# Norm rows through DRAM, scores behind a gate, and two moved steps in a one-core hybrid diffusion step

## The chip, the cores and the metric

The kernel runs on one core of a Trainium2 chip. The metric is the device time of one execution in microseconds; shown are the median and the range of several runs, and one further execution taken with the hardware profiler. The engines are TensorE (PE; its weight loads are listed apart as PEld), VectorE (DVE), ScalarE (ACT), GpSimd (POOL) and SyncE (SP), which issues nearly all DMAs.

## The reference, cut to what matters

One inference step of a two-layer backbone, width 1024, for 128 context tokens and 512 latent tokens that go through the same weights. Layer 0 mixes tokens by a bidirectional chunked scan with 32 heads in 4 groups, layer 1 by differential attention with 8 heads; a gated convolutional channel mixer follows each. All is fp32.

```python
def _rms(x):
    return x * lax.rsqrt(jnp.mean(x * x, axis=-1, keepdims=True) + EPS)

# end of the scan mixer: a norm over each group's 512 channels
y = y.reshape(b, l, SSD_INNER) * jax.nn.silu(z)
y = _rms(y.reshape(b, l, SSD_GROUPS, SSD_INNER // SSD_GROUPS)).reshape(b, l, SSD_INNER)
y = y * norm_g

# differential attention, per head, for a block of 128 queries
s = jnp.einsum('bqhcd,bkhcd->bhcqk', qi, k) * DA_SCALE      # c: two key maps of 64
p = jax.nn.softmax(s, axis=-1)
w = p[:, :, 0] - lam * p[:, :, 1]
o = jnp.einsum('bhqk,bkhd->bqhd', w, v)

# a norm over each head's 128 channels
o = _rms(o) * subln_g * (1.0 - lam_init)
```

Two kinds of norm matter here: that of the four scan groups and that of the eight attention heads. In both, one number per token multiplies all channels.

## The kernel before, in words

Activations lie transposed: channels on the 128 partitions, tokens along the free axis, 640 of them (512 latent, then 128 context). A dense product runs over units of weights: each unit is 128 output channels by 1024 inputs, loaded by SP into one of four raw buffers (L124), split by ScalarE into a rounded high part `whi` (L95) and by VectorE into a low part `wlo` (L101). A tile of 128 outputs takes eight steps of six matmuls (high by high, high by low, low by high, each over two token halves) into one of three wide PSUM buffers, tag "d", of two banks each.

All other work is written as Python generators that are advanced by a tick. Every dense step of six matmuls is a tick (`hook`); a generator that yields n is continued n ticks later. That gives the order in which instructions are written. A planner then orders them once more, outside the stretch at the start that is written under a manual schedule: of the instructions that it thinks ready (operands made, buffer free) an engine takes the one written first. Each engine then executes its own list strictly in that order.

The steps that the change touches:

- `rms_bcast` (L187) makes a norm's factor. Four matmuls of the squares against ones put the sums of 160 tokens each onto partition strips of 32 (tile `ms`); `rsqrt` (L172) takes the root in nine small VectorE operations (`rs_v`, `rs_a`, `rs_y`); after a wait of some ticks four fp32 matmuls against `sel`, columns with the value 0.375 that finish the root's scaling, spread the row to all partitions. The scan's groups write it into the wide buffer `gbc`, the heads into `obc`, the layers' own norms and the first one into `nbc`.
- `ssd_norm` (L877) and the end of `att_tail` (L1084) call it, and VectorE multiplies the data by the spread row and the gains (`svec` columns 16 on, `sg`).
- `att_head` (L1034) forms the scores `sl` of a block of 128 queries: twelve matmuls, six for each of the two key maps, from the high and low parts of q and k. Each map has its own wide buffer, and each uses one half of the array's rows. VectorE takes the maximum, ScalarE the exponential, which frees the buffer.
- `first_tiles` (L380), under the manual schedule, makes the first norm and, in `rows`, products of the condition vector with modulation weights (`modrow`) that arrive by DMA in parts `mp`. The row products of part 0 stand behind the spread of the first root.
- `ssd_dt` (L644) makes the step sizes of the scan and the running sums of the decays. Its rows (`rows`, from `dta`) are written to DRAM as `rowd` and read back, spread over the partitions, as `rb` by each chunk of the scan.

Of the kernel before, what the change touches and what calls it, by code (L numbers as in the profile page):

```python
# [9 lines left out]
F32 = mybir.dt.float32  # L10
# [3 lines left out]
AF = mybir.ActivationFunctionType  # L14
ALU = mybir.AluOpType
# [30 lines left out]
class Step:  # L46
# [140 lines left out]
    def rms_bcast(self, alloc, sq, t0, t1, count, wait=4):  # L187


        n = (t1 - t0) // 4  # L190
        ms = self.bank("m", "ms")
# [5 lines left out]
        self.rsqrt(y, ms[:, :n], n, count)  # L197
        yield wait
        bc = alloc()
        for j in range(4):  # L200
            self.mm(bc[:, j * n:(j + 1) * n], self.sel[:, j:j + 1].to_broadcast([P, P]), y, True, True)
        return bc

    def wide(self, name):
# [175 lines left out]
    def first_tiles(self, h, pool):  # L380
# [243 lines left out]
    def ssd_consts(self, pool):  # L624
        nc, a = self.nc, self.a
        t = lambda shape, name, dt=F32: pool.tile(shape, dt, tag=name, name=name, bufs=1)
        self.scw = t([P, 24, 4], "scw")
        nc.sync.dma_start(self.scw, a["scw"])
        nc.vector.tensor_scalar(self.scw, self.scw, 0.5, None, ALU.mult)
        self.svec = t([P, 32], "svec")  # L630
        nc.sync.dma_start(self.svec, a["svec"])
        self.dtb = t([P, 1], "dtb")
        nc.sync.dma_start(self.dtb, a["dtb"])
        self.fold = t([P, 64], "fold")
        nc.sync.dma_start(self.fold, a["fold"])
        self.ea = t([P, 64], "ea")
        nc.sync.dma_start(self.ea, a["alog"])
        self.act(self.ea, self.ea, AF.Exp)
        self.dt = t([P, NCH, 64], "dt")
        self.C = t([P, NCH, 64], "Ctok")  # L640
        self.wst = t([P, NCH, 64], "wst")
        self.cd = t([P, NCH, 64], "cd")

    def ssd_dt(self, ps):  # L644
# [229 lines left out]
        output(NL, ops)  # L874
        yield 1

    def ssd_norm(self, g, y):  # L877
# [12 lines left out]
    def ssd(self, h, dtps, nextnorm, pool):  # L890
# [4 lines left out]
        def finish(g):  # L895

            yield from self.ssd_group(g, xf[g], *bcs[g], pool)
            scanned[g] = True
            while len(zs[g]) < 4:
                yield 1  # L900
            for t in range(4):
                self.stt(xf[g][t], xf[g][t], 0.5, zs[g][t], ALU.mult, ALU.mult)
            yield 1
            yield from self.ssd_norm(g, xf[g])

        def z_tiles(g):
            for t in range(4):
# [46 lines left out]
    def att_consts(self, pool):  # L954
        nc, a = self.nc, self.a
        t = lambda shape, name, dt=F32: pool.tile(shape, dt, tag=name, name=name, bufs=1)
        self.rope = t([P, 2, TS], "rope")
        nc.sync.dma_start(self.rope, a["rope"])
        lv = t([P, 256], "lv")
        nc.sync.dma_start(lv, a["lam"])  # L960
        ls = t([P, 2], "ls")
        lj = t([P, 64], "lj")
        for i in range(2):
            nc.vector.tensor_tensor_reduce(lj, lv[:, 128 * i:128 * i + 64], lv[:, 128 * i + 64:128 * i + 128], 1.0, 0.0,
                                           ALU.mult, ALU.add, ls[:, i:i + 1])
# [4 lines left out]
        self.sg = t([P, 1], "sg")  # L970
        nc.sync.dma_start(self.sg, a["subg"])
        nc.vector.tensor_scalar(self.sg, self.sg, 1.0 - LAM_INIT, None, ALU.mult)

    def att_v(self, ps, hd, vs, pool):

        nc = self.nc
        x = self.slot("f", f"v{hd}", bufs=NF)
        self.act(x, ps[:, PO:PO + T], AF.Copy)
        hi = pool.tile([P, NCH, P], F32R, tag="vh", name=f"vh{hd}", bufs=2)
        lo = pool.tile([P, NCH, P], F32R, tag="vl", name=f"vl{hd}", bufs=2)  # L980
        vp = pool.tile([P, P], F32, tag="vp", name=f"vp{hd}", bufs=2)
# [14 lines left out]
        self.act(vp, pm[:, :P], AF.Copy)  # L996
        nc.sync.dma_start(self.a["vout"][:, hd * P:(hd + 1) * P], vp)

    def att_evac(self, ps, hd, name, pool):

        x = self.slot("f", f"{name}{hd}", bufs=NF)[:, :TS]
        p = pool.tile([P, TP], F32, tag=f"{name}p", name=f"{name}p{hd}", bufs=2)
        self.act(x, ps[:, PO:PO + TS], AF.Copy)
        self.act(p, ps[:, PO + TS:PO + T], AF.Copy, scale=DA_SCALE if name == "q" else 1.0)
        return x, p

    def att_rope(self, out, x):
# [7 lines left out]
    def att_q(self, x, hd, pool):  # L1015
# [5 lines left out]
        self.stt(lo, q, DA_SCALE, hi.bitcast(F32), ALU.mult, ALU.subtract)  # L1021
        return hi, lo

    def att_k(self, x, hd, pool):

# [5 lines left out]
        self.tt(lo, k, hi.bitcast(F32), ALU.subtract)  # L1031
        return hi, lo

    def att_head(self, hd, qp, kp, qs, k, vs, o, pool):  # L1034


        nc = self.nc
        (qh, ql), (kh, kl) = qs, k
        half = [slice(64 * m, 64 * m + 64) for m in range(2)]

        def softmax(s, n, m, st):
            e = self.slot("f", f"e{m}", bufs=NF)
            nc.vector.tensor_reduce(st[:, m:m + 1], s, AX.X, ALU.max, negate=True)
            self.act(e[:, :n], s, AF.Exp, bias=st[:, m:m + 1], accum_out=st[:, 2 + m:3 + m])
            return e

        def stats():
# [36 lines left out]
    def att_tail(self, hd, w, ws, vs, os_, pool):  # L1084
# [36 lines left out]
        sq = self.slot("sq", "osq", bufs=1)  # L1121
        self.act(sq, o, AF.Square)
        yield 2
        bc = yield from self.rms_bcast(lambda: self.wide("obc"), [sq], 0, T, P, 4 if hd == 7 else 7)
        self.stt(o, o, self.sg, bc[:, :T], ALU.mult, ALU.mult)

    def attention(self, h, nextnorm, pool):
        nc = self.nc
        self.cv = pool.tile([P, D], F32, tag="cv", name="cv", bufs=1)
        nc.sync.dma_start(self.cv, self.a["cv"])  # L1130
        o, tk, self.tails = [], [], {}
# [203 lines left out]
```

## Time and profile before

| | |
|---|---|
| median of 3 runs | 1892.9 us (1892.28 to 1893.92) |
| the profiled execution | 1892.41 us |
| its span, first to last instruction | 1890.6 us |
| mean granted TensorE clock | 0.994 |
| busy share: PE, DVE, ACT | 98%, 73%, 51% |
| DMA, mean over the span | 109 GB/s |

The profile lists for each engine the busy time, then groups of instructions by line, engine, operation and tile, with the idle time before them and what ended it. "out<-in" are the program's names, with the numbers of buffers left out. The chain that ended last follows, from the last instruction back, what released each one. A row of a stretch gives its bounds, its length, the busy time and count of PE, PEld, DVE, ACT and POOL in it, the granted clock, the share of the DMA engines and GB/s; where it is asked of one tile, the busy times are those of the instructions on that tile. A row in order of time gives the start, the length of the merged piece, the engine, the line, the operation and its count.

### The profile page before, as it was taken

What the parts mean: (1) busy time and instruction counts of PE and PEld (TensorE: products, weight loads), DVE (VectorE), ACT (ScalarE), POOL (GpSimd) and SP (SyncE); (2) the same over time, 40 slices, a digit from 0 to 9 for tenths busy, and PEclk for the clock granted to TensorE, in tenths of its full rate; (3) what the DMA queues carried; (4) which work ended last, traced back from release to release, by engine and by line L of the source; (5) the groups of instructions that cost most, each with busy time, mean ns of one, the idle gap of its engine ahead of it and who ended that gap; (6) DMA issues with size and microseconds to landing.
All of it is one profiled execution on the core that took longest, in us unless ns stands there. A gap on an engine that the chain in (4) does not pass through costs nothing.

```text
span 1890.6 us, 32986 instructions
## 1 busy us (share of the span) xinstructions
PE 1857.6 (98%) x13410; PEld 1763.2 (93%) x13410; DVE 1371.1 (73%) x2638; ACT 955.9 (51%) x1748; POOL 0.2 (0%) x4
## 2 busy tenths in 40 slices
PE   7999999999999999999999999999999999999997
PEld 5799999999999999999999988898899999999996
DVE  5689999999658999974455877888686543553554
ACT  3479696968336441442443656666446432441441
POOL 0000000000000000000000000000000000000000
PEclk9999999999999999999999999999999999999998
DMA  9844353526533557632222211111042222222211
GB/s 325 278 115 136 90 155 90 147 91 205 176 113 122 190 169 231 190 102 79 76 70 70 76 49 50 52 35 32 26 124 79 78 72 74 75 72 79 73 40 56
DMA packets 78056, 206.13 MB, mean 109 GB/s; under 512 B 9104, under 2 KB 15824, under 8 KB 77776
## 3 DMA queue, kind: packets, MB, share of 16 engines
q1 hardware_dynamic: 77328, 203.50, 34.3%
q8 instruction: 105, 1.72, 0.4%
q10 hardware_dynamic: 576, 0.52, 0.1%
q14 instruction: 47, 0.39, 0.1%
HBM read 198.06 MB, written 5.93 MB: 108 GB/s over the span
## 4 chain that ended last, share of the span: by engine, by line
PE 94%; DVE 3%; DMA 1%; ACT 1%; SPq 0%; issue 0%; DVEq 0%; ACTq 0%
PE up L104 31%; PE po L104 25%; PE z L104 6%; PE x L104 5%; PE st L104 5%; PE bc L104 3%; PE v L104 3%; PE yp L104 3%; PE q L104 2%; PE sl L104 2%; PE k L104 2%; PE ov L104 1%; PE modrow L104 1%; PE wt L1106 1%; PE in L104 1%; PE xtp L737 1%
## 5 line engine op out<-in xcount | busy, mean ns | idle before, releaser
L95 ACT ACTIVATE whi<-raw 128x1024 fp32r<-128x1024 f32 (+4 forms) x230 | 235.0, 1022 | 406.5 <-PE po L104 237.6
L101 DVE TENSOR_TENSOR wlo<-raw,whi 128x1024 fp32r<-128x1024 f32 (+3 forms) x229 | 269.6, 1178 | 177.4 <-ACT whi L95 171.6
L98 DVE SCALAR_TENSOR_TENSOR xr<-po,mod,xr 128x256 f32<-128x256 f32 (+2 forms) x231 | 88.7, 433 | 157.6 <-PE po L104 157.5
L104 PE MATMUL po<-mh,whi 128*128 128x256 f32 (+1 forms) x704 | 167.6, 310 | 0.0
L104 PE MATMUL po<-ml,whi 128*128 128x256 f32 (+1 forms) x704 | 167.4, 309 | 0.0
L104 PE MATMUL po<-mh,wlo 128*128 128x256 f32 (+1 forms) x704 | 167.1, 309 | 0.0
L104 PE MATMUL up<-h11h,wlo 128*128 128x256 f32 (+1 forms) x656 | 149.4, 309 | 0.0
L104 PE MATMUL up<-h01l,whi 128*128 128x256 f32 (+1 forms) x656 | 149.4, 309 | 0.0
L104 PE MATMUL up<-h11l,whi 128*128 128x256 f32 (+1 forms) x656 | 149.4, 309 | 0.0
L104 PE MATMUL up<-h11h,whi 128*128 128x256 f32 (+1 forms) x656 | 149.4, 309 | 0.0
L104 PE MATMUL up<-h01h,wlo 128*128 128x256 f32 (+1 forms) x656 | 149.4, 309 | 0.0
L104 PE MATMUL up<-h01h,whi 128*128 128x256 f32 (+1 forms) x656 | 149.4, 309 | 0.0
L104 PEld LDWEIGHTS po<-mh,whi 128*128 128x128 f32 x704 | 128.3, 188 | 0.6 <-ACT mh L95 0.4
L104 PEld LDWEIGHTS po<-mh,wlo 128*128 128x128 f32 x704 | 128.5, 188 | 0.0
L104 PEld LDWEIGHTS po<-ml,whi 128*128 128x128 f32 x704 | 128.4, 188 | 0.0
L104 PEld LDWEIGHTS up<-h01h,wlo 128*128 128x128 f32 x656 | 119.3, 188 | 0.0
L104 PEld LDWEIGHTS up<-h01h,whi 128*128 128x128 f32 x656 | 119.3, 188 | 0.0
L104 PEld LDWEIGHTS up<-h11h,wlo 128*128 128x128 f32 x656 | 119.3, 188 | 0.0
L104 PEld LDWEIGHTS up<-h11h,whi 128*128 128x128 f32 x656 | 119.3, 188 | 0.0
L104 PEld LDWEIGHTS up<-h01l,whi 128*128 128x128 f32 x656 | 119.2, 188 | 0.0
L104 PEld LDWEIGHTS up<-h11l,whi 128*128 128x128 f32 x656 | 119.2, 188 | 0.0
L98 DVE SCALAR_TENSOR_TENSOR ca<-uraw,fcw,ca 128x511 f32<-128x511 f32 (+1 forms) x176 | 85.2, 546 | 11.7 <-ACT ca L95 11.7
(496 smaller groups left out, 4385.6 us busy)
## 6 DMA issues: line engine op xcount, KB each, us to landing
raw<-in_w_up SPq DMA_DIRECT2D x88, 512.0 KB, 3.5
mw<-in_modT SPq DMA_DIRECT2D x48, 512.0 KB, 3.6
raw<-in_w_in SPq DMA_DIRECT2D x40, 512.0 KB, 5.1
rb<-rowd SPq DMA_DIRECT2D x40, 512.0 KB, 5.7
raw<-in_w_dn SPq DMA_DIRECT2D x32, 448.0 KB, 3.3
raw<-in_w_qkv SPq DMA_DIRECT2D x24, 512.0 KB, 3.5
mr<-in_mod SPq DMA_DIRECT2D x44, 256.0 KB, 5.3
mp<-in_modp SPq DMA_DIRECT2D x32, 256.0 KB, 5.4
```

The costliest lines, as they stand in the source:

```text
L95: return self.nc.scalar.activation(out, in_, func, **k)
L98: return self.nc.vector.scalar_tensor_tensor(out, in0, s, in1, op0, op1)
L101: return self.nc.vector.tensor_tensor(out, a, b, op)
L104: return self.nc.tensor.matmul(out, lhsT, rhs, start=start, stop=stop)
L737: tr = lambda out, x, c: nc.tensor.transpose(out, x[:, c * P:(c + 1) * P], self.ident)
L1106: nc.tensor.transpose(pm[:, b * P:(b + 1) * P], ws[b][:, kc * P:(kc + 1) * P], self.ident)
```

## The change

Four things are edited.

- A new `rms_spread` takes the place of `rms_bcast` in the four scan groups and in the first seven heads. It writes the row of roots from four partitions to a DRAM row and reads it back to all 128 partitions into an SBUF tile `rbc`; both DMAs are on SP. The factor 0.375 that `sel` had brought goes into the gains (`svec`, and a second column of `sg`; the last head keeps the matmuls and the old gain). The wait before the multiply is 8 ticks in the scan (4 before) and 9 in the attention (7 before).
- In `att_head` the first product of each map and column half of a block is made to depend on the latest copy out of a dense tile, the latest exponential, and the operations that made the low parts of q and k. Blocks start one tick later in all heads but the last.
- In `first_tiles` the row products of the first three of eight steps are written ahead of the spread of the first root.
- In `ssd_dt` the wait ahead of the decay rows is 12 ticks in place of 5.

```diff
+    def rms_spread(self, pool, sq, count, wait):
+
+        n = T // 4
+        y = self.rms_rows(sq, 0, n, count)
+        d = self.dram.tile([T], F32, tag="rsd", name="rsd", bufs=2)
+        self.nc.sync.dma_start(d.rearrange("(j n) -> j n", j=4), y.rearrange("(j r) n -> j r n", r=32)[:, 0, :])
+        bc = pool.tile([P, T], F32, tag="rbc", name="rbc", bufs=1)
+        self.nc.sync.dma_start(bc, d.partition_broadcast(P))
         yield wait
-        bc = alloc()
-        for j in range(4):
-            self.mm(bc[:, j * n:(j + 1) * n], self.sel[:, j:j + 1].to_broadcast([P, P]), y, True, True)
         return bc
...
+        rows(0, 0, 3)
         try:
             next(st)
...
-        rows(0, 0, KT)
+        rows(0, 3, KT)
...
+        nc.vector.tensor_scalar(self.svec[:, 16:], self.svec[:, 16:], 3.0 / 8, None, ALU.mult)
...
-        yield 5
+        yield 12
...
-        bc = yield from self.rms_bcast(lambda: self.wide("gbc"), [sq], 0, T, 512)
+        bc = yield from self.rms_spread(pool, [sq], 512, 8)
...
-        self.act(x, ps[:, PO:PO + T], AF.Copy)
+        self.held["evac"] = self.act(x, ps[:, PO:PO + T], AF.Copy)
...
+    def hold(self, i, gate):
+        for g in gate:
+            self.tc.add_manual_dep(i.ins, g.ins.name, mybir.DependencyInfo(
+                mybir.DependencyClass.Sync, mybir.DependencyReason.DATA), reason="scores")
...
-        yield 3 if last else 4
+        yield 3 if last else 5
...
+            gate = [*self.held.values(), *lows]
...
-                        self.mm(r[:, 192 + c0:192 + c0 + 320], x[hf, qb], kk[hf, c0:c0 + 320], j == 0, j == 2)
+                        i = self.mm(r[:, 192 + c0:192 + c0 + 320], x[hf, qb], kk[hf, c0:c0 + 320], j == 0, j == 2)
+                        if j == 0:
+                            self.hold(i, gate)
...
-        bc = yield from self.rms_bcast(lambda: self.wide("obc"), [sq], 0, T, P, 4 if hd == 7 else 7)
-        self.stt(o, o, self.sg, bc[:, :T], ALU.mult, ALU.mult)
+        if hd == 7:
+            bc = yield from self.rms_bcast(lambda: self.wide("obc"), [sq], 0, T, P, 4)
+        else:
+            bc = yield from self.rms_spread(pool, [sq], P, 9)
+        self.stt(o, o, self.sg[:, hd // 7:hd // 7 + 1], bc[:, :T], ALU.mult, ALU.mult)
```

The remaining edits hand the exponentials, the copies of q and k and the operations of the low parts on, so that `att_head` can name them.

More of the change, by code (lines that the diff above doesn't have):

```diff
@@ L190, in rms_bcast, with rms_rows @@
         n = (t1 - t0) // 4
+        y = self.rms_rows(sq, t0, n, count)
+        yield wait
+        bc = alloc()
+        for j in range(4):
+            self.mm(bc[:, j * n:(j + 1) * n], self.sel[:, j:j + 1].to_broadcast([P, P]), y, True, True)
+        return bc
+    def rms_rows(self, sq, t0, n, count):
         ms = self.bank("m", "ms")
@@ L197, in rms_bcast @@
         self.rsqrt(y, ms[:, :n], n, count)
+        return y
+    def rms_spread(self, pool, sq, count, wait):
[5 more added lines that the diff above has]
+        self.nc.sync.dma_start(bc, d.partition_broadcast(P))
         yield wait
-        bc = alloc()
-        for j in range(4):
-            self.mm(bc[:, j * n:(j + 1) * n], self.sel[:, j:j + 1].to_broadcast([P, P]), y, True, True)
         return bc
@@ L875, in ssd_group, with ssd_norm @@
         yield 1
-    def ssd_norm(self, g, y):
+    def ssd_norm(self, g, y, pool):
         sq = self.slot("sq", "gsq", bufs=1)
@@ L903, in finish @@
             yield 1
-            yield from self.ssd_norm(g, xf[g])
+            yield from self.ssd_norm(g, xf[g], pool)
         def z_tiles(g):
@@ L969, in att_consts @@
         nc.vector.tensor_scalar(self.nlam, self.nlam, -LAM_INIT, None, ALU.add)
-        self.sg = t([P, 1], "sg")
-        nc.sync.dma_start(self.sg, a["subg"])
-        nc.vector.tensor_scalar(self.sg, self.sg, 1.0 - LAM_INIT, None, ALU.mult)
+        self.sg = t([P, 2], "sg")
+        nc.sync.dma_start(self.sg[:, 1:], a["subg"])
+        nc.vector.tensor_scalar(self.sg[:, 1:], self.sg[:, 1:], 1.0 - LAM_INIT, None, ALU.mult)
+        nc.vector.tensor_scalar(self.sg[:, :1], self.sg[:, 1:], 3.0 / 8, None, ALU.mult)
     def att_v(self, ps, hd, vs, pool):
@@ L1003, in att_evac @@
         self.act(x, ps[:, PO:PO + TS], AF.Copy)
-        self.act(p, ps[:, PO + TS:PO + T], AF.Copy, scale=DA_SCALE if name == "q" else 1.0)
+        self.held["evac"] = self.act(p, ps[:, PO + TS:PO + T], AF.Copy, scale=DA_SCALE if name == "q" else 1.0)
         return x, p
@@ L1020, in att_q @@
         self.act(hi, q, AF.Copy, scale=DA_SCALE)
-        self.stt(lo, q, DA_SCALE, hi.bitcast(F32), ALU.mult, ALU.subtract)
-        return hi, lo
+        i = self.stt(lo, q, DA_SCALE, hi.bitcast(F32), ALU.mult, ALU.subtract)
+        return hi, lo, i
     def att_k(self, x, hd, pool):
@@ L1030, in att_k @@
         self.act(hi, k, AF.Copy)
-        self.tt(lo, k, hi.bitcast(F32), ALU.subtract)
-        return hi, lo
+        i = self.tt(lo, k, hi.bitcast(F32), ALU.subtract)
+        return hi, lo, i
     def att_head(self, hd, qp, kp, qs, k, vs, o, pool):
         nc = self.nc
-        (qh, ql), (kh, kl) = qs, k
+        (qh, ql, i), (kh, kl, j) = qs, k
+        lows = i, j
         half = [slice(64 * m, 64 * m + 64) for m in range(2)]
@@ L1043, in softmax @@
             nc.vector.tensor_reduce(st[:, m:m + 1], s, AX.X, ALU.max, negate=True)
-            self.act(e[:, :n], s, AF.Exp, bias=st[:, m:m + 1], accum_out=st[:, 2 + m:3 + m])
+            self.held["exp"] = self.act(e[:, :n], s, AF.Exp, bias=st[:, m:m + 1], accum_out=st[:, 2 + m:3 + m])
             return e
@@ L1130, in attention @@
         nc.sync.dma_start(self.cv, self.a["cv"])
-        o, tk, self.tails = [], [], {}
+        o, tk, self.tails, self.held = [], [], {}, {}
         self.start_tiles(h)
```

## The prediction, made before the result was known

> **What bounds the kernel now.** I read the busy totals and the chain that ended last first, then the busy time by stretch of the stages that the change touches, then single tiles and the order in time around each edit.
>
> ```profile
> span 1890.6 us, 32986 instructions
> PE 1857.6 (98%) x13410; PEld 1763.2 (93%) x13410; DVE 1371.1 (73%) x2638; ACT 955.9 (51%) x1748; POOL 0.2 (0%) x4
> PE 94%; DVE 3%; DMA 1%; ACT 1%; SPq 0%; issue 0%; DVEq 0%; ACTq 0%
> ...
> 84.00:100.00 16.00, 16.00 (x114) 14.33 (x113) 7.00 (x12) 9.14 (x20) 0.00 (x0) 1.00 0.76 275
> ...
> 60.00:490.00 430.00, 428.29 (x3308) 391.14 (x3307) 393.54 (x798) 322.53 (x755) 0.00 (x0) 1.00 0.48 143
> 1040.00:1330.00 290.00, 288.13 (x1968) 257.58 (x1968) 227.53 (x471) 178.23 (x375) 0.00 (x0) 0.99 0.16 48
> ```
>
> TensorE carries 94% of the chain, and in the two stages that the change edits (the scan, 60 to 490 us; the attention, 1040 to 1330 us) it is busy all but 1.7 and 1.9 us. A microsecond of TensorE work taken out there is a microsecond of the time, unless VectorE, 78% busy in the attention and 92% in the scan, becomes late. So I count TensorE time and then look for what VectorE's order could give back.
>
> **Part 1, the spread of the norm rows.** Today four matmuls against `sel` copy the row of roots to 128 partitions, in eight passes, and a wide PSUM buffer holds the result until VectorE has read it.
>
> ```profile
> L104 PE MATMUL gbc<-rs_y,cst x32: 297/299/375, 209.2 to 492.0; 128*128 128x160 f32 x32
> L104 PE MATMUL obc<-rs_y,cst x64: 298/299/403, 1123.0 to 1364.5; 128*128 128x160 f32 x64
> ...
> 1159.78 1.25 PE L104 MATMUL obc<-rs_y,cst 128*128 128x160 f32 x8
> 1160.76 0.44 PE L104 MATMUL k<-h10l,whi 128*128 128x384 f32 x1
> ...
> 1123.04 1.35 PE L104 MATMUL obc<-rs_y,cst 128*128 128x160 f32 x8
> 1124.12 0.44 PE L104 MATMUL k<-h10l,whi 128*128 128x384 f32 x1
> ```
>
> From the start of one spread to the next matmul it is 0.98 us at 1159.78 and 1.08 us at 1123.04, so 1.03 us each. The 32 passes of gbc are four spreads and go; of the 64 of obc, eight spreads, seven go, since the last head keeps the matmuls. 11 x 1.03 = **11.3 us** less TensorE work. The four `ms` products and the nine small VectorE operations of the root stay. The multiply that follows reads SBUF in place of PSUM; it is the same operation, I cost it at nothing. The two scalings by 3/8 are two tiny VectorE operations in start-up code; the same VectorE has idle time there, so nothing.
>
> Added per spread: a small write to DRAM and a broadcast read of 320 KB, both on SP's queue, and the read waits for the write to land. The nearest rows are the scan's own pair of this kind, `rowd` and `rb` (512 KB).
>
> ```profile
> rb<-rowd SPq DMA_DIRECT2D x40, 512.0 KB, 5.7
> rowd<-rows_s SPq DMA_DIRECT2D x2, 80.0 KB, 1.8
> k<-in_ck SPq DMA_DIRECT2D x8, 64.0 KB, 3.3
> DMA to landing us min/median/max: 4.8/5.7/11.0
> ...
> 1148.08 0.48 PE L104 MATMUL ms<-osq,cst 128*32 128x160 f32 x8
> 1153.63 0.31 DVE L98 SCALAR_TENSOR_TENSOR rs_y<-rs_a,rs_y 128x160 f32<-128x160 f32 x1
> ...
> 200.36 0.48 PE L104 MATMUL ms<-gsq,cst 128*32 128x160 f32 x8
> 203.71 0.32 DVE L98 SCALAR_TENSOR_TENSOR rs_y<-rs_a,rs_y 128x160 f32<-128x160 f32 x1
> 209.20 1.25 PE L104 MATMUL gbc<-rs_y,cst 128*128 128x160 f32 x8
> ```
>
> The last two figures of the fourth line are the median and the slowest landing of `rb`. Between the bounds 3.3 us (the 64 KB read) and 5.7 us I take 4.5 for 320 KB; with 1.8 us for the write and an estimated 0.8 us for two issues the row is there 7.1 us after the root. In the attention the spread now stands seven ticks behind `ms`, 1159.78 - 1148.08 = 11.7 us, 1.67 a tick; nine ticks are 15.0, so the multiply is due at 1163.1, 9.2 us after the root ends at 1153.9. In the scan four ticks took 209.20 - 200.36 = 8.8 us; eight, if the added ones take half as long as these (1.1 us each), give 13.2, so 9.5 us after the root's end at 204.0. The row is there 2 to 3 us early in both, and I charge **nothing**; without that cover each late microsecond stands on VectorE, which works in order. Where the root itself ends late (the last group of the scan) I charge 1 us.
>
> Behind SP's wait for the write queue the weight loads.
>
> ```profile
> 1151.83 0.33 SPq L124 DMA_DIRECT2D raw<-in_w_qkv  x1
> raw<-in_w_qkv SPq DMA_DIRECT2D x24, 512.0 KB, 3.5
> ```
>
> There are four raw buffers: a load goes into the one that a cast has just freed and is itself cast four weight units later, and a head (1159.78 - 1123.04 = 36.7 us) uses three. It lands in 3.5 us. SP held for the root and for the landing, some 2 to 8 us, is hidden by that lead.
>
> **Part 2, the scores.** A block has twelve matmuls, six for each of two key maps, that use one half of the array's rows each; a pair side by side runs together.
>
> ```profile
> sum 176.00, PE 49.95 PEld 38.42 DVE 46.30 ACT 44.66; mean PE 6.24 PEld 4.80 DVE 5.79 ACT 5.58
> ...
> 1144.00:1147.00 3.00, 1.14 (x12) 0.88 (x12) 0.80 (x2) 0.00 (x0) 1.00 0.02 5
> 1151.00:1153.00 2.00, 1.65 (x12) 1.39 (x12) 0.00 (x0) 0.00 (x0) 1.00 0.06 12
> 1155.00:1158.00 3.00, 1.79 (x12) 1.52 (x12) 0.94 (x2) 1.37 (x4) 1.00 0.00 1
> ...
> 1187.77 0.56 PE L104 MATMUL sl<-kh,qh 64*128 64x320 f32 x2
> 1188.17 0.30 PE L104 MATMUL sl<-kl,qh 64*128 64x320 f32 x1
> 1188.29 0.41 PE L104 MATMUL sl<-kh,qh 64*128 64x320 f32 x1
> ...
> PEld sl L104 <- ACT e L95: 3.4, 13, 0.8
> ```
>
> The first line is the score tile `sl` alone, summed over eight stretches, one a head: 49.95 us for 32 blocks. A block in the written order takes 1.14 us; where one map's PSUM buffer came free before the other's, the planner started that map alone (two products of map one, then a third of another kind, at 1187.77) and the block takes 1.65 or 1.79. At 1.14 all would take 36.5, so 13.5 us can go. The new dependencies make every first product of a block wait for both buffers and both low parts, so the planner can no longer start half a block. Two blocks of a head's four are now broken by just that. But part of the excess in the first and last heads is the half clock, which the run may have anywhere, and a held block starts up to one exponential later, in a stage where PE now waits at most 0.8 us for it. Bounds: -13.5 and, if the order stays, 0; I take **-10** for the order, nearest to the rows of the regular heads, and **+2** for new waits (the 3.4 us seen now, half again). The tick that moves the blocks (4 to 5) is hidden by the dense tiles beside it.
>
> The Trainium skill (TensorEngine Tiling (Array Packing), section Theoretical Speedup) says up to 2x for a contraction of at most 64; this trace has 1.79 against 1.14, or 1.6x. By that rule the scores would fall by 25 us instead of 10, an estimate from that page, and the sum would be 1856.
>
> **Part 3, three products ahead of the root's spread** at the start.
>
> ```profile
> 9.77 5.86 SPq L392 DMA_DIRECT2D mp<-in_modp  x8
> mp<-in_modp SPq DMA_DIRECT2D x32, 256.0 KB, 5.4
> 17.13 2.10 PEld L104 LDWEIGHTS nbc<-rs_y,cst 128*128 128x128 f32 x8 [3.79 <-DVE rs_y L98]
> 17.14 2.50 PE L104 MATMUL nbc<-rs_y,cst 128*128 128x160 f32 x8 [3.23 <-DVE rs_y L98]
> 19.57 3.64 PE L104 MATMUL modrow<-mp,s 128*32 128x128 f32 x64
> 25.23 1.12 PE L104 MATMUL in<-h00h,whi 128*128 128x256 f32 x4 [1.30 <-ACT h00h L95]
> ```
>
> PE idles 3.2 us before the spread. Loads are issued every 0.73 us from 9.77, so the third lands near 11.2 + 5.4 = 16.6. Three of the eight steps are 24 of 64 passes, 24 x 57 ns = 1.37 us; the last of them ends about 17.1, when the root is there. The row sum behind the spread, which the first dense matmul at 25.23 waits for, ends 1.37 us sooner: **-1.4 us**. Had the third load come 1 us later, the spread would wait and about 0.4 remain.
>
> **Part 4, decay rows later** (wait 5 to 12).
>
> ```profile
> PE rows L104 <- DVE dta L101: 1.7, 1, 1.7
> 84.02 1.12 SPq L734 DMA_DIRECT2D rb<-rowd  x2
> L104 PE MATMUL yp<-m,xt x320: 272/273/324, 129.4 to 476.2; 128*64 128x128 f32 x160
> ```
>
> TensorE waits 1.7 us for `dta`; seven ticks later it has long been made: **-1.7 us**. All that follows in that task moves by about 7 us: the row sums' copy, its two writes on SP, the three small products and `rb` (84.02 to about 91). The task now takes 31 of the 32 ticks that the first group's four dense tiles give, so nothing is drained in a hurry. The first use that TensorE waits for is at 129.4, some 38 us behind; that is the cover. If it failed the 7 us would show in full, so the bounds are -1.7 and +5.
>
> **Sum.** 1892.4 (the profiled execution: span 1890.6 and 1.8 around it; the median of the runs shown is 1892.9, 0.03% above) - 11.3 + 1 - 10 + 2 - 1.4 - 1.7 = **1871**, which is 1.1% faster. 0.2%, 3.8 us, is about what can be told from no change.
>
> **The rivals.**
> - The scores keep their cost: the planner still splits blocks, or what is won is lost in waits of TensorE for the held products. For it speaks that TensorE takes its instructions in order and a held block waits with everything behind it; against it, that TensorE has dense work to put ahead and waits little there now. Without the -10 the sum is 1881.
> - Slower: the broadcast rows come late and VectorE, in order, stands in front of the multiply, with the reductions, the casts and with them the PSUM buffers behind it. The slowest `rb` took 11.0 us. With that the row is there 13.6 us after the root, 4.4 late in seven heads and 4.1 in four groups, 47 us in all; all passed on to TensorE, 1918. It decides from 21.4 / 11 = 1.9 us a spread. For it: VectorE is 92% busy in the scan. Against: that 11.0 stands at 84 us, where the DMA engines are crowded (share 0.76 in the stretch from 84 to 100 us, the second last figure of its row), while the attention's share is 0.16.
> - It doesn't do what it says, no change: VectorE sets the pace in scan and attention as soon as TensorE is lightened, so that Parts 1 and 2 vanish and only 3.1 us of the start stay: 1889.3. For it the 92%; against it the 78% and that VectorE's idle time in the scan is still 36 of 430 us, far above the 4.1 us taken out there.
> - The pairs run at twice the speed of a single map's products, half of 1.79, 0.9 us a block: 32 blocks take 28.6, 21.4 us less than now in place of 10: 1860. Against it, no block in the trace takes under 1.14. The packing rule of the Trainium skill named above points this way.
>
> **How the numbers follow.** The forecast, 1871, has 0.60, with its own range from 1864 (all 13.5 of the scores, no new waits, the last group not late) to 1879 (some 2 of the scores' 10). Scores unchanged, 1881: 0.20. Late rows, 1918: 0.11. No change: 0.05. Pairs at double speed, 1860: 0.04. Faster is the first, second and last, 0.84; same 0.05; slower 0.11. The range from 1860 to 1887 takes in the forecast, the unchanged scores with 6 us of the bounds of Parts 3 and 4 and of the late last group, and the pairs at double speed; what it leaves out is late rows and no change, 0.16.
>
> **What would show it.** Part 1: no gbc, obc only in the last head, and DVE's multiply by the spread row waiting for nothing; a wait of DVE on a DMA of that row of more than 1 us each shows the slower rival. Part 2: the score tile's sum near 37 us over the same stretches, in groups of twelve, each about 1.1, with the pair order kept; its waits on ACT under 6 us. A sum still near 50 is the first rival. Part 3: 24 passes of the row product before 17 us, and the first dense matmul near 23.9. Part 4: no wait of `rows` for `dta`, `yp` no later than before. TensorE still near 98% busy with a shorter span says that its work was the bound; a share that falls with VectorE's rising over 85% in the attention says that the bound moved. The prediction is wrong if the planner, which now orders by other readiness, puts dense tiles elsewhere and their buffers collide; nothing in the trace prices that.

## The result, and the profile after

The changed kernel takes 1887.2 us (median of 9 runs, 1884.46 to 1888.75) against 1892.3 us before (9 runs, 1890.79 to 1893.92): 0.9972 of the time, 95% interval 0.9962 to 0.9983. It is faster, by 5 us and not by the 21 of the forecast, and it ends just above the range. The profiled execution's span is 1884.7 us. Of all executions below one is left out of the ratios, one of ahead-decay that took 5031.6 us.

The first lines of the page, after:

```profile
span 1884.7 us, 32852 instructions
...
PE 1839.6 (98%) x13322; PEld 1744.8 (93%) x13322; DVE 1369.5 (73%) x2640; ACT 955.1 (51%) x1748; POOL 0.2 (0%) x4
...
PE 90%; DVE 5%; ACT 3%; DMA 2%; issue 1%; SPq 0%; DVEq 0%; ACTq 0%
```

TensorE's busy time fell by 18.0 us, the span by 5.9. In the chain TensorE has 90% in place of 94%, VectorE and ScalarE together 8% in place of 4%. Which stage lost it is seen in the stretches of the prediction, here after (the columns as there), and below them one row of the kernel before for some five regular heads of the attention:

```profile
1110.00:1290.00 180.00, 171.11 (x1185) 151.12 (x1183) 136.15 (x272) 108.04 (x227) 0.00 (x0) 0.98 0.17 53
1040.00:1330.00 290.00, 271.86 (x1864) 241.16 (x1862) 222.81 (x446) 176.14 (x367) 0.00 (x0) 0.97 0.17 52
60.00:490.00 430.00, 429.46 (x3311) 393.83 (x3310) 396.39 (x805) 325.19 (x760) 0.00 (x0) 1.00 0.49 148
```

```profile
1110.00:1290.00 180.00, 179.89 (x1259) 161.66 (x1258) 141.20 (x284) 110.41 (x233) 0.00 (x0) 1.00 0.15 47
```

The scan is as full as before (0.5 us of idle time). In the attention TensorE now idles 18.1 of 290 us where it idled 1.9, and does fewer instructions in the same time: from 1110 to 1290 us 1185 in place of 1259, and only 40 of the 74 that are missing belong to the spreads. Yet the score tile did shrink. Its busy time from 1040 to 1370 us, which holds all 384 products, before and after:

```profile
1040.00:1370.00 330.00, 50.52 (x384) 38.73 (x384) 50.27 (x64) 54.39 (x128) 0.99 0.15 45
```

```profile
1040.00:1370.00 330.00, 40.48 (x384) 31.00 (x384) 50.31 (x64) 54.70 (x128) 0.97 0.17 52
```

So 10 us of scores and 7 us of spreads went, and waits came. What TensorE waited for in the attention, after, from 1040 to 1330 us (us, times, longest):

```profile
PE v L104 <- ACT e L95: 5.5, 6, 0.9
PE wt L1136 <- ACT wpT L95: 4.8, 6, 1.4
PE sl L104 <- ACT e L95: 4.5, 8, 2.9
PE sl L104 <- ACT kp L95: 1.9, 1, 1.9
```

The place, in order of time in one regular head, after:

```profile
1150.14 0.46 PE L104 MATMUL k<-h10l,whi 128*128 128x256 f32 x2
1150.79 0.57 PE L104 MATMUL sl<-kh,qh 64*128 64x320 f32 x4 [0.19 <-ACT e L95]
...
1151.87 0.56 PE L104 MATMUL k<-h10h,wlo 128*128 128x256 f32 x2
1152.27 0.27 PE L1119 MATMUL wpt<-cst,wp 128*128 128x128 f32 x1
1153.22 0.55 PE L1136 MATMUL wt<-cst,w 128*128 128x128 f32 x3 [0.68 <-ACT wpT L95]
1154.68 0.56 PE L104 MATMUL v<-h10h,whi 128*128 128x256 f32 x2 [0.91 <-ACT e L95]
```

The fourth block of a head starts two dense products before the end of the `k` tile. Its two maps and `k` hold all three wide buffers, so `v` can start only when an exponential has freed one. The planner has nothing left to place but `wpt` and three `wt`, and the `wt` wait for ScalarE's copy of what `wpt` gave. From 1151.87 to 1154.68 TensorE does at most 1.4 us of work in 2.8 (the rows' 0.56, 0.27 and 0.55). Before, 15 products of `k`, the spread and three more products stood behind that block.

The chain that ended last says the same. The kernel before, from 1149.63 (start, length, what):

```profile
1149.63 1.77 PE k L104 x12
1151.41 1.58 PE sl L104 x11
1152.99 2.85 PE k L104 x18
1155.85 1.72 PE sl L104 x11
1157.56 2.38 PE k L104 x15
1159.94 1.09 PE obc L104 x8
```

After, from 1147.09:

```profile
1147.09 0.80 DVE w L98
1147.88 0.24 DVE rs_a L101
1148.12 0.73 DVE sm L1070
1148.85 0.23 DVE rs_a L98
1149.08 0.75 DVE sm L1070
...
1152.89 0.83 DVE sm L1070
1153.71 0.02 issue
1153.74 0.90 ACT e L95 x2
1154.63 0.04 issue
1154.68 1.44 PE v L104 x8
```

Before, this part of the chain is TensorE alone. After, it runs through VectorE's maxima (`sm`), which stand in line behind the combination of the weights (`w`) and the root (`rs_a`), and through the exponentials (`e`), to the start of `v`.

### The profile page after: what moved, and what is told of

Read it like the earlier page. It is cut to its first block, busy times and chain, and to the rows that moved or that the text cites. A ratio compares the mean times of both kernels' runs of the same rounds, so it can differ in the third digit from the quotient of the medians.

```text
span 1884.7 us, 32852 instructions
## 1 busy us (share of the span) xinstructions
PE 1839.6 (98%) x13322; PEld 1744.8 (93%) x13322; DVE 1369.5 (73%) x2640; ACT 955.1 (51%) x1748; POOL 0.2 (0%) x4
## 4 chain that ended last, share of the span: by engine, by line
PE 90%; DVE 5%; ACT 3%; DMA 2%; issue 1%; SPq 0%; DVEq 0%; ACTq 0%
PE up L104 31%; PE po L104 25%; PE z L104 6%; PE x L104 5%; PE st L104 5%; PE yp L104 3%; PE v L104 3%; PE q L104 3%; PE bc L104 3%; PE ov L104 1%; ACT e L95 1%; PE modrow L104 1%; PE in L104 1%; PE sl L104 1%; DVE sm L1070 1%; PE wt L1136 1%
```

## The experiments

Ratios are to the kernel before, measured beside each run; 0.001 is 1.9 us, and a difference between two such ratios is uncertain by some 0.0015 to 0.002, 3 to 4 us. "Spread" is the spread by transfers, "hold" the new dependencies of the scores, "tick" the wait ahead of the blocks (4 before, 5 in the change), "tail" the task with `wpt`, `wt` and `ov`.

**Hold and tick taken apart.** Theory A: hold and tick together put the fourth block at the end of `k`. Theory B: the held products themselves are late. Theory C: late rows on VectorE. Four kernels beside the changed one: the old tick with the hold, no hold with the new tick, neither (the spread alone is left in the attention), and a tick of 3.

```diff
tick4, nohold-tick4:
-        yield 3 if last else 5
+        yield 3 if last else 4
tick3:
-        yield 3 if last else 5
+        yield 3
nohold, nohold-tick4:
-                        if j == 0:
-                            self.hold(i, gate)
```

> The changed kernel with one number undone: blocks of scores start 4 ticks behind the context scores again, not 5; the dependencies of the scores and all else stay. Measured is the way from the first up product of layer 0 to that of layer 1, 837.4 us in the kernel before and 842.0 in the changed one. Theory A (the tick and the dependencies together put the fourth block at the end of the k tile; both its buffers are taken when v wants one, the planner has only wpt and wt left to place, and TensorE waits there and loses clock): with 4 ticks, 10 to 12 products of k stand behind the fourth block, the waits of wpt, wt and v, 21 us in the changed kernel, shrink to under 4, no half clock in the regular heads; way 826 to 830, time 1870 to 1876. Theory B (the held products themselves cost the time: every block waits for exponentials): way 839 to 842, time 1884 to 1888.

> The changed kernel without the dependencies of the scores, 5 ticks kept. Theory A: the third or fourth block is split again, so a buffer comes free for v half a block sooner; the waits of wpt, wt and v go, the scores cost 44 to 49 us again instead of 39: way 830 to 836, time 1876 to 1882. Theory B: all of the loss goes with the dependencies and the scores cost what they cost before: way 826 to 830, time 1870 to 1876; under B this one is faster than the run with 4 ticks, under A slower.

> The changed kernel without Part 2 altogether: no dependencies of the scores, 4 ticks; the norm rows still by DMA. Both theories: the scores cost about 48 us as before and the seven spreads are gone, so the way is 837.4 less 7.2 (seven spreads in the attention) = 830 if the rows arrive in time. Over 834 would say that the rows by DMA cost something in the attention; that is theory C, late rows.

> The changed kernel with 3 ticks in place of 5, dependencies kept. Theory A: the fourth block moves further from the end of the k tile (19 products of k behind it), the waits of wpt, wt and v stay under 4 us: way 825 to 831, within 2 us of the run with 4 ticks. Theory B: as with 5 ticks, 839 to 842.

| | time, us | ratio | interval |
|---|---|---|---|
| tick4 | 1888.1 | 0.9972 | 0.9962 to 0.9983 |
| nohold | 1887.2 | 0.9971 | 0.9959 to 0.9982 |
| nohold-tick4 | 1885.6 | 0.9960 | 0.9945 to 0.9975 |
| tick3 | 1893.6 | 1.0005 | 0.9995 to 1.0014 |

None of A's numbers came. The old tick with the hold (tick4) is no better than the changed kernel, so the tick alone isn't it: there 12 products of `k` stand behind the fourth block, and `v` waits all the same. With the new tick and no hold, only score products wait. Waits of TensorE in the attention, first one of tick4's, then the only one listed for nohold:

```profile
PE v L104 <- ACT e L95: 4.4, 6, 0.9
```

```profile
PE sl L104 <- ACT e L95: 3.4, 8, 1.2
```

So `v` waits with the hold, whichever the tick, and not with the tick alone. B's number came for tick4 to 0.1 us, but not for nohold, and tick3 is slower than either theory had it: products of other tiles break up its blocks in spite of the hold (the score tile takes 49.4 us), and TensorE idles 10.5 of 290 us. Without hold and tick the kernel gains 7.6 us, some 6 short of the 13.4 that start, scan and spread were to bring in the forecast (3.1 + 3.1 + 7.2). The ways that the expectations speak of, 837.4 us before, are 840.8 (tick4), 840.0 (nohold), 837.7 (nohold-tick4) and 847.0 us (tick3). C's sign, over 834 us in nohold-tick4, did come, but not its cause: VectorE waits nowhere for the row there, so C falls. The attention of nohold-tick4 is full of work again, and no shorter. Some five regular heads in that kernel, then its score tile, and then the start of one head in order of time:

```profile
1110.00:1290.00 180.00, 179.84 (x1203) 155.22 (x1203) 137.50 (x276) 108.67 (x230) 0.00 (x0) 1.00 0.17 55
```

```profile
1040.00:1370.00 330.00, 54.56 (x384) 39.87 (x384) 50.25 (x64) 54.50 (x128) 0.99 0.17 52
```

```profile
1204.39 0.41 PE L104 MATMUL sl<-kh,qh 64*128 64x320 f32 x2
1204.73 0.50 PE L104 MATMUL ov<-wTh,vh 128*128 128x512 f32 x1
1205.16 0.41 PE L104 MATMUL sl<-kh,qh 64*128 64x320 f32 x1
1205.17 0.56 PE L104 MATMUL sl<-kl,qh 64*128 64x320 f32 x3
1205.65 0.66 PE L1134 MATMUL wt<-cst,w 128*128 128x128 f32 x4
```

With the spreads gone, the planner sends the tail of one head into the first score block of the next. The pairs break there, the score tile grows from 50.5 to 54.6 us, which is 4.1 of the 7.2 us that the spreads left free, and busy time no longer measures work done. Where the other 3 went, and why nohold doesn't gain the 7.2 us, is not shown.

**Is TensorE's work the bound of the attention at all?** Theory D: yes, and the new order lost the gain. Theory E: no, a head's 36 to 37 us come from the chain of maximum, exponential and buffer. The kernel before with each of seven spreads made twice; the changed kernel with TensorE's spread in the attention (hold and tick stay); the scan's spread and the start alone, with the attention of before; the start alone.

```diff
obc-twice, from before:
-        for j in range(4):
+        for j in [*range(4)] * twice:
...
hold-mm, from the change:
-            bc = yield from self.rms_spread(pool, [sq], P, 9)
...
+        bc = yield from self.rms_bcast(lambda: self.wide("obc"), [sq], 0, T, P, 4 if hd == 7 else 7)
scan-start: hold-mm, without the hold, tick 4
ahead-decay, from before:
+        rows(0, 0, 3)
...
-        rows(0, 0, KT)
+        rows(0, 3, KT)
...
-        yield 5
+        yield 12
```

> The kernel before, with each spread of the root in the attention's first seven heads made twice (eight products of the same kind into the same buffer): 7 x 1.03 = 7.2 us more work for TensorE, the planner's order otherwise nearly that of before (two wt products move up by two dense products). Theory D: in the attention a microsecond of TensorE work is a microsecond of the time, and the changed kernel lost its gain to the new order alone; then 1892.6 + 7.2 = 1899.8. Theory E: a head's period of some 36 to 37 us is set by a chain through the scores' buffers, VectorE's maxima and ScalarE's exponentials, in which TensorE has slack, so that work taken out or put in there hardly shows; then at most 2 us more, 1892.6 to 1894.6.

> The changed kernel, but the attention's root is spread by TensorE again, as before; the held scores, the later tick, and the scan's and the start's parts stay. 7.2 us more TensorE work in the attention than in the changed kernel. Theory D: 1887.2 + 7.2 = 1894.4. Theory E: within 2 us of the changed kernel, 1885 to 1889; four products of the spread now stand between the products that wait, so part of the waits is filled.

> Only the scan's spread by transfers, the three row products ahead and the later decay rows; the attention is that of before, order and spread included. The forecast's own terms give 4 x 1.03 - 1 + 1.4 + 1.7 = 6.2 us less, 1886.4; the positions of the first up product in the traces so far (7 to 10 us earlier) give 1882.6 to 1885.6. If this is as fast as the run with the spread alone in the attention (1885.6), the attention's part of the spread is worth nothing (Theory E); if Theory D holds and only the new order cost that run its gain, both come out alike too, so this run measures the other parts and is read together with the two above.

> The kernel before with the start's two parts alone: three row products ahead of the root's spread, and the decay rows seven ticks later. The forecast's terms: 1.4 + 1.7 = 3.1 us less, 1889.5. The position of the dense products in the changed kernel's trace (4.8 us earlier after the first tiles, 6.8 after the decay rows, part of it a stretch of half clock that the trace of before has at 27 us and that of the changed kernel lacks) would give 1885.8 to 1888 if the half clock is of the start's order, and 1889.5 if it is chance.

| | time, us | ratio | interval |
|---|---|---|---|
| obc-twice | 1897.5 | 1.0036 | 1.0023 to 1.0049 |
| hold-mm | 1890.3 | 0.9995 | 0.9985 to 1.0004 |
| scan-start | 1883.0 | 0.9961 | 0.9948 to 0.9974 |
| ahead-decay | 1887.3 | 0.9978 | 0.9968 to 0.9987 |

7.2 us more work cost 6.8 us (interval 4.4 to 9.3): TensorE is the bound of the attention before, and Theory E falls as a statement on that kernel. hold-mm ends between D's 1894.4 and E's 1885 to 1889. The four runs split the change. The start is worth 4.2 us, the scan's spread 3.2 (0.9978 to 0.9961). The attention's spread alone, scan-start to nohold-tick4, is worth nothing (0.9961 and 0.9960). Hold and tick on top of scan-start cost 6.4 us (0.9961 to 0.9995), which is clear of the uncertainty; the spread beside them gives 4.4 back (0.9995 to 0.9972). scan-start, which leaves the attention as it was, has the lower ratio of the two, 0.9961 to the whole change's 0.9972, though the intervals overlap.

**The order tested by one tick of the tail, and by a shorter maximum.** Theory F: work and order on TensorE decide. The tail starts one tick later, with hold and tick (tail3) and without (spread-tail3). In the other two the maximum of a map is taken over the first half of the keys: a part of that work is left out, and the softmax keeps its value.

```diff
tail3, from the change; spread-tail3, from nohold-tick4:
-        self.tails[hd] = self.add(self.att_tail(hd, w, ws, vs, o, pool), 1 if last else 2)
+        self.tails[hd] = self.add(self.att_tail(hd, w, ws, vs, o, pool), 1 if last else 3)
half-max-scan, from scan-start; half-max-spread, from nohold-tick4:
-            nc.vector.tensor_reduce(st[:, m:m + 1], s, AX.X, ALU.max, negate=True)
+            nc.vector.tensor_reduce(st[:, m:m + 1], s[:, :n // 2], AX.X, ALU.max, negate=True)
```

> The changed kernel with one number changed: a head's tail (the transposes of the weights wpt and wt and the products ov) starts one tick later in all heads but the last (3 for 2). In the written order the four wt of a chunk then stand together behind 24 dense products, in place of three of them right behind wpt. Theory F: the held scores and the spread do save their 7 + 10 us of TensorE work, and the changed kernel lost them because wpt and wt stand where no dense tile has a buffer; then their start-to-start time falls back from 7.7 + 25.4 towards 0.6 + 15 us, and the time from 1887 to 1870 to 1876. Theory E (a head's period is set by VectorE and ScalarE through the scores' buffers): the waits turn up elsewhere and the time stays within 3 us of the changed kernel, 1884 to 1890.

> The same edit of the tail on the kernel without held scores and with the old tick (spread by transfers, start as changed; 1885.6). There the wt and ov of a head break into the first score block of the next. Theory F: the score blocks stay whole again, 3 to 7 us less, 1878 to 1883. Theory E: within 2 us of 1885.6.

> The kernel with the scan's spread and the start's parts only (1883.0), with VectorE's maximum of each score map taken over the first half of the keys (the shift of the exponential changes, the softmax does not; a part of the maximum is left out). VectorE has some 0.35 us less in each of 10 reductions a head, 3 us a head, and the exponential starts earlier. TensorE's work is the same. Theory E: the period of a head falls by 1 us or more, 1873 to 1878. Theory F (TensorE's work and its order are the bound): 1881 to 1885.

> The same shorter maximum on the kernel with the spread by transfers in scan and attention, no held scores and the old tick (1885.6). The shorter maximum also moves the planner's order: the first block of a head is no longer broken up. Theory E: 8 us less or more, 1874 to 1878, heads near 35.5 us. Theory F: what the order brings, 2 to 7 us less, 1878 to 1884, and with whole blocks the spread's 7.2 us begin to show against the run above.

| | time, us | ratio | interval |
|---|---|---|---|
| tail3 | 1888.0 | 0.9976 | 0.9966 to 0.9985 |
| spread-tail3 | 1879.9 | 0.9933 | 0.9918 to 0.9948 |
| half-max-scan | 1881.7 | 0.9943 | 0.9926 to 0.9959 |
| half-max-spread | 1874.1 | 0.9904 | 0.9889 to 0.9919 |

Without the hold, one tick of the tail gives 5 us, as F has it, and now the attention's spread seems to show: 0.9961 to 0.9933, 5.3 of its 7.2 us. No run has the tail's tick without the spread, so part of the 5.3 may be the tick's own. spread-tail3 beats both kernels, by 12.7 us the one before. The score tile's row of that kernel is back below that of before:

```profile
1040.00:1370.00 330.00, 48.82 (x384) 35.08 (x384) 51.13 (x64) 55.58 (x128) 0.99 0.18 56
```

With the hold the same tick gives nothing: F's number for tail3 was missed by 12 us, and E's came. There `wt` waits once and no longer six times, but `v` waits twice as long for the exponential. Waits of TensorE in tail3:

```profile
PE v L104 <- ACT e L95: 10.9, 6, 1.9
...
PE wt L1136 <- ACT wpT L95: 1.4, 1, 1.4
```

The shorter maximum takes 3.4 us off where TensorE has the spread to do (within the uncertainty), and 10.6 where it hasn't: with TensorE lightened, a step of VectorE counts. E's number came for half-max-spread, F's for half-max-scan. Both kernels also got another order, so this is no clean price of the maximum. With the shorter maximum in both, the attention's spread shows in full: 0.9943 to 0.9904, 7.4 us.

**Where the hold loses.** Theory G: it makes the fourth block late. Theory H: only the later tick did harm. The full hold on the best kernel with the old tick; the hold on three of four blocks; the changed kernel with the shorter maximum (the same part left out as above).

```diff
hold-best, from spread-tail3:
-            gate = []
+            gate = [*self.held.values(), *lows]
hold-three, from spread-tail3:
-            gate = []
+            gate = [*self.held.values(), *lows] if b < 3 else []
```

> The kernel with spread by transfers, old tick and later tail (1879.9), with the held scores of the change added and nothing else. In the planned order the fourth block moves from 18 to 10 products before the end of the k tile. Theory G (the hold puts the fourth block late, and the next dense tile waits for its exponentials): the scores shrink by some 8 us, but waits of v for the exponential come back, and the time is 1884 to 1890. Theory H (only the later tick did harm): the pairing is won, 1870 to 1874.

> The same, but only the first three blocks of a head are held; the fourth may be split as before and stands 16 products before the end of k, with 12 of v behind. Theory G: no wait of v for the exponential, part of the pairing won, 1874 to 1878. If any hold costs as much as it brings: 1879 to 1884.

> The changed kernel with the maximum of each score map taken over the first half of the keys (part of the maximum is left out, the softmax does not change): the exponentials, and with them the buffers, come some 0.35 us earlier for each map, and the planner puts the fourth block 22 dense products, not 2, ahead of wpt. Theory G: waits of wt for wpT and of v for the exponential go, 10 to 15 us less than the changed kernel, 1872 to 1877. If the waits were due to something else than the fourth block's release: the shorter maximum alone is worth some 1.5 us, as in the scan-only kernel, 1885.

| | time, us | ratio | interval |
|---|---|---|---|
| hold-best | 1882.3 | 0.9946 | 0.9931 to 0.9961 |
| hold-three | 1882.6 | 0.9948 | 0.9931 to 0.9965 |
| half-max-after | 1879.7 | 0.9931 | 0.9916 to 0.9946 |

hold-best ends between G's and H's numbers. Its score tile and its longest sum of waits:

```profile
1040.00:1370.00 330.00, 40.53 (x384) 29.94 (x384) 50.78 (x64) 55.38 (x128) 0.99 0.18 54
```

```profile
PE v L104 <- ACT e L95: 4.6, 6, 0.9
```

Eight microseconds less of scores than in spread-tail3, and the time is no shorter. hold-three has no such wait of `v`, but its unheld fourth block splits, its score tile takes 49.9 us, and nothing is won either: G's number was missed, and the other one, 1879 to 1884, came. In half-max-after the waits of `wt` for `wpT` and of `v` fall to 0.4 and 1.3 us and the time by 7.8 us against the change, in direction as G has it, 2 to 7 us short of its size. It is still 5 us slower than half-max-spread, which has neither hold nor tick (0.9931 to 0.9904).

**The first head.** In hold-best the first head takes 28.9 us from its first `sp` to the next head's, in spread-tail3 23.7. So the hold from the second head on, and the best kernel once more beside it:

```diff
hold-later, from hold-best:
-            gate = [*self.held.values(), *lows]
+            gate = [*self.held.values(), *lows] if hd else []
```

> The kernel of hold-best with the first head's blocks not held. In hold-best that head took 28.9 us from its first score product to the next head's, 23.7 without the hold. If the hold itself costs that, 5 us less than hold-best, 1876 to 1879, and the regular heads stay near 36.5 us; if the loss only moves on to the second head, 1880 to 1883.

> The kernel of spread-tail3 once more, beside the one above: 1878 to 1881, regular heads 35.5 us. If the hold is worth anything outside the first head, the run above is faster than this one.

hold-later took 1881.1 us (0.9940, 0.9927 to 0.9952), spread-tail3b 1880.2 us (0.9938, 0.9924 to 0.9951). The first head takes 26.5 us in hold-later and 26.7 in spread-tail3b, so the two executions of the kernel without the hold differ by 3 us themselves there, and the first head explains nothing about the hold. The clock explains those 3 us: from 1072 to 1080 us the mean granted clock is 0.57 in spread-tail3b and 1.00 in spread-tail3. A regular head takes 36.5 us in hold-best and hold-later and 35.5 us in both executions without the hold. The whole is the same within the uncertainty. The hold brought no gain in any order that was tried. The waits of `v` and `wt` show, for the changed kernel, tail3, tick4 and hold-best, that a late fourth block and its exponentials take much of the gain; whether an order exists in which whole blocks pay is open.

## Why the prediction was wrong, step by step

**Parts 3 and 4: right, and a little small.** Forecast 3.1 us, measured 4.2 (interval 2.5 to 6.1). After, in order of time:

```profile
14.42 2.01 PE L104 MATMUL modrow<-mp,s 128*32 128x128 f32 x24 [1.32 <-DMA mp<-in_modp]
16.35 2.05 PE L104 MATMUL nbc<-rs_y,cst 128*128 128x160 f32 x8
18.33 1.30 PE L104 MATMUL modrow<-mp,s 128*32 128x128 f32 x40
...
21.90 1.12 PE L104 MATMUL in<-h00h,whi 128*128 128x256 f32 x4 [1.54 <-ACT h00h L95]
```

The 24 passes fill the idle time, and the spread starts without a wait. The first dense matmul comes at 21.90, not at the 23.9 forecast: the root was there 0.8 us sooner (16.35, before 17.14; 16.41 in ahead-decay), and with 40 passes left the first dense matmul follows 3.57 us behind their start, where with 64 it took 5.66 (25.23 - 19.57): 2.1 us saved for the 1.37 forecast. The wait of `rows` for `dta` is gone, and `yp` starts at 122.6 in place of 129.4.

**Part 1, the scan: right.** 4 x 1.03 - 1 = 3.1 us forecast, 3.2 measured, uncertain by some 3. **The rows' arrival: the charge of nothing holds and the slower rival falls, though the cover was smaller than worked out.** After, the transfers of the row, VectorE's waits for them in the whole run, and the landing (min/median/max):

```profile
rbc<-rsd SPq DMA_DIRECT2D x11, 320.0 KB, 3.4
  DMA rbc<-rsd: 1.5, 2
DMA to landing us min/median/max: 3.4/3.4/3.4
```

The estimate was 4.5 us. The landing is on record for only two of the eleven reads, both in the scan. In the head shown above the read is issued at 1151.66 and the multiply starts at 1155.56, 5.5 us after the root's end at 1150.05 where 9.2 were forecast. A landing of 3.4 us leaves a cover of 0.5 us, not 2 to 3: the multiply came earlier than worked out, the row too, and that the two errors cancelled was luck.

**Part 1, the attention: the sentence "A microsecond of TensorE work taken out there is a microsecond of the time" failed in one direction.** Work put in costs its length (6.8 of 7.2 us). Work taken out gave 0, 4.4, 5.3 or, with the shorter maximum, 7.4 of 7.2 us, each uncertain by 3 to 4, as the planner's order fell out. Its exception, that VectorE "becomes late", is what happened in the changed kernel, at 77% busy (222.81 of 290 us): VectorE was not full, it had the wrong thing in front at the moment that decided. In nohold-tick4 it is not what happened: there TensorE is full, and about half of the gain, by busy time, went into broken blocks.

**Part 2: the failed term.** The "-10 for the order" came in full, 50.5 to 40.5 us of the score tile. "+2 for new waits" is the step that broke: 16.7 us in the waits shown above, where TensorE idled 1.9 in all before. The term was built on one row, the wait of the scores' weight loads for the exponential, 3.4 us before. That row grew by 3.8 us, near enough:

```profile
PEld sl L104 <- ACT e L95: 7.2, 11, 3.2
```

What it put at nothing are the waits of the products behind the held block, `v` and `wt`, 10.3 us. The hold moves the fourth block late in the `k` tile, and the next tile has no buffer. The tick, of which the prediction says that it "is hidden by the dense tiles beside it", makes this worse in the changed kernel: `k` ends two products behind that block, and TensorE idles 18.1 of 290 us where it idles 12.8 in tick4. But it isn't the cause: with the old tick and the hold (tick4, hold-best) `v` waits too, and with the new tick alone (nohold) it doesn't. Part 2 as a whole was forecast at -8 and measured at +6.4 (scan-start to hold-mm). With -4.2 for the start, -3.2 for the scan and -4.4 for the attention's spread that makes the 5.3 us that the change is faster, but for rounding. The last sentence of the prediction named this mechanism and left it without a price or a chance. The first rival, waits in place of the -10, named the right kind of loss and 10 of the 16 us, but looked for it at the held products. A bound could have been had: three wide buffers, two of them a block's, the third the tile's, so whatever is left of the tile behind the last block must cover at least a maximum and an exponential (0.8 + 0.9 us, from the chain's rows). That is too low: from the block's end to `v` it is 2.8 us in the changed kernel (1151.87 to 1154.68), since VectorE first ends what stands in front.

**The pairs at double speed: did not come.** A held block takes 1.08 us (1150.79 to 1151.87), the same as a whole block before. By the Trainium skill (TensorEngine Tiling (Array Packing), section Theoretical Speedup) up to 2x is possible; no run here shows more than the 1.6 of the prediction's rows.

## What to carry to other kernels

Before an edit that takes work off the bounding engine, count for each buffer rotation what stands between the last use of a buffer and its next one; the removed work may be the cover. Where a planner orders the instructions, look at the new order around the edit first and then try one tick to either side: here the spread of seven rows was worth nothing in one order and some 5 us, in part perhaps the tick's own, with a neighbouring task one tick later. Measure the parts of a change one by one, since a good part (the start, the scan, 7 us) can hide a bad one.

## What was not expected of the hardware

The granted clock halves in short stretches within the attention of the changed kernel, in regular heads where the kernel before has 1.00. One of two such stretches (the other is at 1267 us), and one in the first head, where the kernel before has a shorter one, after:

```profile
1192.00:1195.00 3.00, 3.00 (x13) 3.00 (x12) 3.00 (x8) 1.61 (x5) 0.00 (x0) 0.50 0.51 163
1072.00:1082.00 10.00, 6.17 (x32) 5.21 (x33) 9.20 (x14) 5.60 (x12) 0.00 (x0) 0.53 0.19 59
```

Over 1040 to 1330 us the mean clock is 0.97 after and 0.99 before, which over 290 us is at most some 6 us at full speed (an estimate, 3 to 9 by the rounding; TensorE idled for part of it), about a third of the 16 us by which the gain fell short. It is not only the profiled execution: the nine executions of the changed kernel have mean clocks of 0.990 to 0.994, and the one at 0.994 is the fastest, 1884.46 us. tail3, with the longest waits, has 0.97 in the stretch from 1110 to 1290 us, the changed kernel 0.98 there. hold-mm, whose waits are as long as the changed kernel's, has 1.00 there, so waits alone don't bring the half clock. In the 3.4 us ahead of 1192.0 TensorE is busy for 1.80 us. The least that a regular head has in 3.4 us is 3.3 us before and some 2.5 in tick4 and hold-best, and none of these has the half clock there; but hold-mm goes down to 1.80 us and has none either. What sets it off is open.
